# One accumulation over all blocks for layer 1's expert outputs, with four PSUM banks held for it

## The chip, the cores and the metric

One core of one Trainium2 chip runs the whole program. The metric is device time in microseconds (us), one execution of the kernel from start to end; lower is better. Everything is float32 (partly in the float32r form that the TensorE takes at its quicker rate), and the profile names the engines PE (TensorE's matmuls), PEld (its weight loads), DVE (VectorE), ACT (ScalarE), POOL (GpSimd) and SP (the queue that issues nearly all weight loads from memory).

## What is computed

Two layers of a transformer over 256 tokens and 256 context tokens of width 1024. Each layer is modulation, attention, an output projection with a layer norm, then a mixture of experts (MoE) with a second layer norm. In layer 1 only the 256 tokens are left. The part that matters here, cut to its core:

```python
def moe(h, w_router, b_router, w_gate, w_up, w_down):
    ...   # 16 experts in 4 groups; each token picks the best group and its top 2 experts, with weights `gates`
    g = jnp.einsum('...d,edf->...ef', h, w_gate)
    u = jnp.einsum('...d,edf->...ef', h, w_up)
    a = jax.nn.silu(g) * u * gates[..., None].astype(h.dtype)
    return jnp.einsum('...ef,efd->...d', a, w_down)

x = layer_norm(ALPHA * x + g2 * moe(h2, ...), ln_g[l, 1], ln_b[l, 1])
```

## The kernel before

**Blocks.** The kernel doesn't compute all experts for all tokens. Each expert has a slot with a capacity (CAPS, line 39), each slot is cut into blocks of 128, 64 or 32 rows (cut, line 53), and a block computes its expert for the tokens that were routed to it. Layer 1 has 13 slots: three static ones of 32 rows, then ten dynamic ones of 192, 32, 32, 64, 64, 96, 128, 64, 32 and 32 rows in that order, 15 blocks in all (192 is 128 + 64, 96 is 64 + 32). Expert weights (gate, up and down, 2 MB each) come through a ring of twelve tiles of 1 MB; a load is issued on SP when the tile's earlier contents have been used by PE. A loop behind it (overflow, line 1534) takes rows that no slot had room for; here its condition is false and it is skipped.

**One block of layer 1** (step, line 1449) is, in program order: products (line 1226: gate and up products into the PSUM role "acc", L1247 for 32 or 64 rows, L1232 and L1234 for 128), copied out by ACT (L1250); hidden (line 1253: PE transposes through PSUM role "tr", L234; a sigmoid on ACT, L1270; two multiplications on DVE, L1271 and L1272, the second of which writes aT); flush, which is put (line 1331) of the block before; down (line 1275: the product of aT with the down weights into "acc", L1290 or L1284); and put_out's steps (DVE L1326, ACT L1327, DVE L1328) that scale the rows and split them into a high and a low part, yh and yl. The next block's products follow on PE without a wait for these.

**put** scatters a block's rows back to the 256 tokens with matmuls. dt is a one-hot matrix (DVE, L1339, one buffer), and for each of two token tiles t and two column halves n it takes a bank of PSUM role "c" (two buffers), adds the products with yh and yl in it (L1346), and adds the bank to the token rows xs on DVE (L1349). So each block has four such additions, 15 blocks have 60, and the third group of a put waits until the first bank has been read.

**Look-ups and picking.** Which tokens a block takes is found by ranks: block_index (line 1146) makes one-hot matrices dd on DVE (L1159, two buffers), multiplies them on PE into PSUM role "ix" (look_up, L1172) and copies the result out (L1179, L1180). This is done in five batches, the last three (4, 6 and 2 blocks) beside the first blocks. pick (line 1298) gathers up to 128 tokens for a group of blocks with matmuls through "tr" (L1311), copied out by ACT (L1313).

**What sets the order.** The program is not run in the order written: a scheduler at build time orders each engine's instructions by program position among those that it takes to be ready, and gives out a tile's buffers as they come free in its own estimate of time. On the chip each engine then runs its list in order. PSUM has eight banks. In layer 1's MoE the roles hold "acc" 3, "tr" 2, "ix" 1 and "c" 2 (phase, line 191).

Of the kernel before, what the change touches and what calls it, by code (L numbers as in the profile page):

```python
# [10 lines left out]
F32R = mybir.dt.float32r  # L11
# [10 lines left out]
P = 128  # L22
# [120 lines left out]
class K:  # L143
# [47 lines left out]
    def phase(self, kind):  # L191

        if self.c_pp:
            self.c_pp()
        g = self.tc.tile_pool(name=f"pp{self.npp}", bufs=1, space=PSUM)
        self.npp += 1
        self.pp = g.__enter__()
        self.c_pp = lambda: g.__exit__(None, None, None)
        if kind == "attn":
            self.pmap = {"s": ("s", 2), "s2": ("s", 1), "tr": ("tr", 2), "o": ("o", 1), "acc": ("acc", 2), "m": ("m", 1)}  # L200
        else:
            self.pmap = {"acc": ("acc", 4), "tr": ("tr", 3), "ix": ("ix", 1)} if kind == "moe0" else \
                {"acc": ("acc", 3), "tr": ("tr", 2), "ix": ("ix", 1), "c": ("c", 2)}

    def warm(self, n, role, after=None, mark=None):

# [1121 lines left out]
            nc.vector.tensor_sub(yl[:, cs], t, yh[:, cs])  # L1328
        return (yh, yl), out

    def put(self, ys, R, tok, T):

        nc = self.nc
        W = D * R // P
        nj = P // R
        m = self.const(f"jm{R}")
        dt = self.sp.tile([P, nj, P * T], F32R, name="dt", tag="dt", bufs=1)
        for j in range(nj):
            nc.vector.tensor_scalar(dt[:, j], self.const("iota")[:, 0:P * T], tok, m[:, j:j + 1], op0=ALU.is_equal, op1=ALU.mult)  # L1339
        for t in range(T):  # L1340
            for n in range(2):
                ps = self.psum([P, 512], "c")
                w = min(W, 512)
                for c in range(512 * n, 512 * n + 512, w):
                    for i in range(2):
                        nc.tensor.matmul(ps[:, c % 512:c % 512 + w], dt[:, c // W, P * t:P * t + P], ys[i][:, c % W:c % W + w],  # L1346
                                         start=i == 0, stop=i == 1, skip_group_check=True)
                x = self.xs[:, t, 512 * n:512 * n + 512]
                nc.vector.tensor_add(x, x, ps)  # L1349

    def moe(self, l, T, h2d, yd, rp, prep):

        nc = self.nc
# [6 lines left out]
        def onehots(blks):  # L1360

            n = sum(R for _, _, R in blks)
            dd = self.sp.tile([P, T, n], F32R, name="ddr", tag="ddr", bufs=2)
            o = 0
            for sc, r0, R in blks:
                nc.vector.tensor_tensor(dd[:, :, o:o + R], self.const("iota")[:, r0:r0 + R][:, None, :].to_broadcast([P, T, R]),
                                        self.rt["Rs"][:, :, sc:sc + 1].to_broadcast([P, T, R]), op=ALU.is_equal)
                o += R
            return dd
# [59 lines left out]
                    n += R  # L1429
            return out  # L1430

        todo, held = [], []

        def run1(grs, xt0=None, last=False):

            for g in grs:
                xt, xt0 = xt0 or self.pick(onehots([x[:3] for x in g]), T), None
                while todo:
                    step()
                o = 0  # L1440
                for sc, r0, R, load in g:
                    todo.append((xt[:, :, o:o + R], R, load))
                    o += R
            while last and todo:
                step()
            if last:
                flush()

        def step():
            xt, R, load = todo.pop(0)  # L1450
# [8 lines left out]
            self.down(aT, R, wd, out)  # L1459
            held.append((y, R, x))  # L1460

        def flush():
            while held:
                self.put(*held.pop(0), T)

        NS = NE - ndyn(l)
        early = [self.expert_load(l, *s[:2]) for s in slots[:NS]] if l else []
# [6 lines left out]
        n = self.block_index(l, T, slots[:1], 0, ixs)  # L1474
        if l == 0:
            self.warm(3, "acc", self.looked)
        n = self.block_index(l, T, slots[1:NS], n, ixs)
# [3 lines left out]
        if l:  # L1481
            run1(gs, xt0)
        else:
            run(slots[:NS])
            settle()
        self.route_b(l, T, rp)
        for lo, hi in ((NS, NS + 3), (NS + 3, NS + 8), (NS + 8, len(slots))) if l else ((NS, NS + 2),):
            n = self.block_index(l, T, slots[lo:hi], n, ixs)
        if l:
            self.route_c(l, T, rp)  # L1490
            while len(todo) > KEEP:
                step()
            run1(gd, last=True)
            return
# [3 lines left out]
        for j, (lo, hi) in enumerate(zip(cuts, cuts[1:])):  # L1498

            up = min(hi + 3, len(slots))  # L1500
            if up > seen:
                n = self.block_index(l, T, slots[seen:up], n, ixs)
# [31 lines left out]
    def overflow(self, l, T, h2d, yd, prep):  # L1534

        tc, nc, a = self.tc, self.nc, self.a
# [4 lines left out]
        tok = self.const(f"tok{l}", T, 4 + 2 * l)  # L1541
        iota = self.const("iota")
        with tc.If(v > 0):
# [3 lines left out]
            with tc.For_i(0, NE, 1) as e, tc.tile_pool(name=f"ov{l}", bufs=2) as vp:  # L1547
                fl = vp.tile([1, T], I32, name="fl")
                nc.sync.dma_start(fl, fid[bass.ds(e, 1)])
                for b in range(T):  # L1550
                    fv = nc.values_load(fl[0:1, b:b + 1], min_val=0, max_val=512)
                    with tc.If(fv > 0):
                        rs = vp.tile([P, T, T], F32, name="rs")
                        nc.sync.dma_start(rs.rearrange("p b t -> p (b t)"), rod[bass.ds(e, 1)].rearrange("o p x -> (o p) x"))
                        kk = vp.tile([P, T], F32, name="kk")
                        nc.sync.dma_start(kk, k2d[bass.ds(e, 1)].rearrange("o p t -> (o p) t"))
                        rh = vp.tile([P, T, 4 + 2 * l], BF, name="rh")
                        nc.vector.tensor_copy(rh, tok)
                        if l == 0:
                            self.second(rh[:, :, 3:4], kk[:, :, None], T)  # L1560
                        else:
                            k3 = vp.tile([P, T], F32, name="k3")
                            self.pieces(lambda i: rh[:, :, 1 + 2 * i], kk, k3)
                        dd = vp.tile([P, T, P], BF, name="dd")
                        eq = (iota[:, 0:P][:, None, :].to_broadcast([P, T, P]), rs[:, b][:, :, None].to_broadcast([P, T, P]))
                        nc.vector.tensor_tensor(dd, *eq, op=ALU.is_equal)
                        pi = self.psum([P, 1, 2], "ix")
                        self.look_up(pi[:, 0, :], dd, rh, T, l)
                        ix = [vp.tile([P, 1], F32 if l else I32, name=f"ix{i}") for i in range(2)]
                        if l == 0:  # L1570
                            self.finish_index(l, *ix, pi, None, None)
                            xg = vp.tile([P, D], F32, name="xg", bufs=1)
                            nc.vector.memset(xg, 0.0)
                            self.gather(xg, ix[0], P, h2d, NT)
                            xt = self.xgT(xg, P)
                        else:
                            self.finish_index(l, *ix, pi, None, None)
                            ddr = self.sp.tile([P, T, P], F32R, name="ddr", tag="ddr", bufs=2)
                            nc.vector.tensor_tensor(ddr, *eq, op=ALU.is_equal)
                            xt = self.pick(ddr, T)  # L1580

                        def part(nm):
                            kp = 4 if nm == "w_down" else 8
                            n = 4096 // kp
                            rows = "(k p)" if nm == "w_down" else "(p k)"
                            s = a[nm][l][bass.ds(e, 1)].rearrange(f"o {rows} f -> p (o k) f", p=P)

                            def get(k):
                                w = self.ep.tile([P, n], F32, name="wv" + nm, tag="xt" if kp == 4 else "gu")
                                nc.sync.dma_start(w, s[:, k, :])  # L1590
                                return w
                            return get
                        aT = self.hidden(self.products(xt, P, part("w_gate"), part("w_up")), P)
                        wd = part("w_down")
                        y, out = self.rows_out(P) if l == 0 else self.put_out(P, ix[1])
                        pss = [self.psum([P, 512]) for _ in range(2)]
                        for k in range(4):
                            w = wd(k)
                            for n in range(2):
                                nc.tensor.matmul(pss[n], aT[:, k, :], w[:, 512 * n:512 * n + 512], start=k == 0, stop=k == 3)  # L1600
                        for n in range(2):
                            out(pss[n], slice(512 * n, 512 * n + 512))
                        if l == 0:
                            self.scatter(y, ix[1], P, yd, NT)
                        else:
                            self.put(y, P, ix[0], T)

    def combine_load(self, t, T, yd):
        NT = P * T
# [277 lines left out]
```

## Time and profile before

| what | value |
|---|---|
| median of 3 runs | 1063.53 us (1056.98 to 1065.07) |
| the profiled execution | 1061.43 us, its span 1059.6 us |
| PE busy over the span | 979.2 us, 92% |
| DVE busy over the span | 507.3 us, 48% |
| ACT busy over the span | 259.9 us, 25% |
| HBM traffic | 272 GB/s over the span |

The span is the time from the first to the last profiled instruction; what lies around it is 1.8 us. The profile is one execution. PE's busy time has modelled ends, because matmuls overlap in the pipeline: the distance from one start to the next tells what a matmul costs, and a gap before a matmul together with the engine that ended it tells what PE waited for. The granted clock (PEclk) is TensorE's clock as a share of its full 2.4 GHz. Layer 1's MoE lies at the end, from about 820 us to 1047 us of the span.

### The profile page before, as it was taken

The numbers are of one execution on the slowest core, as the hardware profiler recorded it, in microseconds if no ns is written. First come the engines' busy times: TensorE is split into PE (matmuls) and PEld (weight loads), VectorE is DVE, ScalarE is ACT, GpSimd is POOL, SyncE is SP. The second block draws the span as 40 slices with busy tenths as digits, with TensorE's granted clock in tenths as the row PEclk, the third lists the DMA queues.
The fourth block names the chain that finished last, engine by engine and source line by source line (L and its number), as shares of the span: only waits on it lengthen the run. The fifth ranks groups of instructions, "written<-read, shape, count | busy, mean of one in ns | idle before, by whom it ended". The sixth has DMA issues, their size and how long they took to land. (4 is left out here: it accounts for less than half of the span.)

```text
span 1059.6 us, 15578 instructions
## 1 busy us (share of the span) xinstructions
PE 979.2 (92%) x5918; PEld 533.2 (50%) x5918; DVE 507.3 (48%) x1368; ACT 259.9 (25%) x685; POOL 86.0 (8%) x90
## 2 busy tenths in 40 slices
PE   4799999989899899999999997998999999999994
PEld 1466557667544444544444443443653665544542
DVE  2524555665747833331100105879838742533346
ACT  2433343553412111101111211423413111111110
POOL 0000000000102303111111110111003000000001
PEclk9799999999999999999999899999999889999997
DMA  8899761201265199997999986769634692999991
GB/s 313 298 350 330 258 214 58 80 24 57 105 239 214 63 392 401 408 414 292 390 402 401 358 301 248 315 245 405 263 140 136 252 418 79 417 418 376 363 353 47
DMA packets 76937, 286.99 MB, mean 271 GB/s; under 512 B 12449, under 2 KB 27441, under 8 KB 55604
## 3 DMA queue, kind: packets, MB, share of 16 engines
q1 hardware_dynamic: 71600, 268.13, 65.4%
q0 software_dynamic: 4272, 15.08, 4.0%
q10 hardware_dynamic: 980, 2.66, 0.6%
q8 instruction: 51, 0.84, 0.3%
q14 instruction: 34, 0.28, 0.1%
HBM read 279.77 MB, written 8.69 MB: 272 GB/s over the span
## 5 line engine op out<-in xcount | busy, mean ns | idle before, releaser
L1247 PE MATMUL acc<-wring,xt 128*32 128x256 f32 (+1 forms) x1440 | 140.2, 436 | 0.5 <-ACT xt L1223 0.5
L1247 PEld LDWEIGHTS acc<-wring,xt 128*32 128x32 f32 (+1 forms) x1440 | 59.0, 118 | 73.1 <-issue 49.7
L855 PE MATMUL acc<-wring,oT 128*128 128x512 f32 x192 | 89.2, 598 | 0.3 <-DVE y L857 0.3
L1290 PE MATMUL acc<-wring,aT 128*32 128x256 f32 (+1 forms) x720 | 70.7, 436 | 6.5 <-DVE aT L1272 4.2
L459 PE MATMUL acc<-swh,hT 128*128 128x384 f32 x192 | 68.2, 355 | 3.9 <-ACT v L581 3.5
L460 PE MATMUL acc<-swl,hT 128*128 128x384 f32 x192 | 67.6, 352 | 0.0
L1349 DVE TENSOR_TENSOR xs<-xs,c 128x512 f32<-128x512 f32 x60 | 40.4, 684 | 54.6 <-PE c L1346 54.5
L461 PE MATMUL acc<-swh,hT 128*128 128x384 f32 x192 | 66.2, 345 | 0.0
L523 PE MATMUL acc<-wring,hT 128*128 128x512 f32 x128 | 58.8, 593 | 0.0
L1284 PE MATMUL acc<-wring,aT 128*128 128x512 f32 x128 | 57.1, 597 | 0.5 <-DVE aT L1261 0.4
L1232 PE MATMUL acc<-wring,xt 128*128 128x512 f32 x128 | 56.7, 596 | 0.0
L1234 PE MATMUL acc<-wring,xt 128*128 128x512 f32 x128 | 56.2, 592 | 0.0
L410 PE MATMUL m<-wring,cT 128*32 128x512 f32 x256 | 44.3, 660 | 12.4 <-DMA wring<-in_w_mod_dram 12.4
L855 PEld LDWEIGHTS acc<-wring,oT 128*128 128x128 f32 x192 | 33.9, 190 | 33.0 <-issue 31.4
L1290 PEld LDWEIGHTS acc<-wring,aT 128*32 128x32 f32 (+1 forms) x720 | 27.8, 117 | 38.1 <-issue 20.7
L370 POOL TENSOR_TENSOR mv<-ve,nhalf 128x1 f32<-128x1 f32 x12 | 18.3, 1529 | 330.9 <-DVE ve L369 263.6
L1250 ACT COPY gu<-acc 128x256 f32<-128x256 f32 (+1 forms) x27 | 12.0, 444 | 122.5 <-PE acc L1247 122.5
L459 PEld LDWEIGHTS acc<-swh,hT 128*128 128x128 f32 x192 | 36.4, 189 | 9.5 <-issue 4.5
L1234 PEld LDWEIGHTS acc<-wring,xt 128*128 128x128 f32 x128 | 24.3, 190 | 30.6 <-issue 30.4
L1232 PEld LDWEIGHTS acc<-wring,xt 128*128 128x128 f32 x128 | 23.8, 190 | 28.3 <-issue 27.6
L461 PEld LDWEIGHTS acc<-swh,hT 128*128 128x128 f32 x192 | 36.3, 189 | 3.0 <-issue 3.0
L460 PEld LDWEIGHTS acc<-swl,hT 128*128 128x128 f32 x192 | 36.4, 190 | 2.4 <-issue 2.4
(354 smaller groups left out, 1527.9 us busy)
## 6 DMA issues: line engine op xcount, KB each, us to landing
wring<-in_w_gate_dram SPq DMA_DIRECT2D x58, 1024.0 KB, 14.4
wring<-in_w_up_dram SPq DMA_DIRECT2D x58, 1024.0 KB, 15.3
wring<-in_w_down_dram SPq DMA_DIRECT2D x58, 1024.0 KB, 14.2
wring<-in_w_mod_dram SPq DMA_DIRECT2D x48, 1024.0 KB, 8.1
wring<-in_w_in_even_dram SPq DMA_DIRECT2D x24, 256.0 KB, 4.4
wring<-in_w_in_odd_dram SPq DMA_DIRECT2D x6, 1024.0 KB, 11.4
wring<-in_w_out_even_dram SPq DMA_DIRECT2D x4, 1024.0 KB, 5.1
wring<-yd SPq DMA_DIRECT2D x4, 1024.0 KB, 5.8
```

What stands on the lines that cost most here:

```text
L410: nc.tensor.matmul(ps[32 * j:32 * j + 32, :], lhs(k), w[k][:, 512 * j:512 * j + 512], start=k == 0, stop=k == len(w) - 1, tile_position=(0 ...
L459: mm(ps, xh, wh, start=first, stop=False)
L460: mm(ps, xh, wl, start=False, stop=False)
L461: mm(ps, xl, wh, start=False, stop=last)
L523: self.nc.tensor.matmul(ps, h[:, k, :], w(k), start=k == 0, stop=k == 7)
L855: mm = nc.tensor.matmul(ps, oT[:, k, P * t:P * t + P], w[n](k), start=k == 0, stop=k == 7)
L1232: nc.tensor.matmul(pg, xt[:, k, :], gate(k), start=k == 0, stop=k == 7)
L1234: nc.tensor.matmul(pu, xt[:, k, :], up(k), start=k == 0, stop=k == 7)
L1247: nc.tensor.matmul(ps[R * j:R * j + R, :], xt[:, k, :], src[:, W * jj:W * jj + W], start=k == 0, stop=k == 7, tile_position=(0, R * j), sk ...
L1284: nc.tensor.matmul(ps, aT[:, k, :], w(k)[:, 512 * n:512 * n + 512], start=k == 0, stop=k == 3)
L1290: self.last_mm = nc.tensor.matmul(ps[R * j:R * j + R, :], aT[:, k, :], w(k)[:, W * j:W * j + W], start=k == 0, stop=k == 3, tile_position= ...
L1349: nc.vector.tensor_add(x, x, ps)
```

## The change

Layer 1's put no longer takes a bank for each product and adds it to xs. The first put takes four banks (two token tiles by two halves), every later put adds its products to the same four, and only the last put closes them and adds them to xs, with four additions in all. To pay for it "c" gets four banks, "acc" goes from three to two, and "ix" loses its own bank: look-ups take the two banks of "tr". The one-hot matrix dt gets a second buffer. Layer 0 and the overflow path compute as before.

```diff
-                {"acc": ("acc", 3), "tr": ("tr", 2), "ix": ("ix", 1), "c": ("c", 2)}
+                {"acc": ("acc", 2), "tr": ("tr", 2), "ix": ("tr", 2), "c": ("c", 4)}
...
-    def put(self, ys, R, tok, T):
+    def put(self, ys, R, tok, T, sums, last):
...
-        dt = self.sp.tile([P, nj, P * T], F32R, name="dt", tag="dt", bufs=1)
+        dt = self.sp.tile([P, nj, P * T], F32R, name="dt", tag="dt", bufs=2)
...
+        first = not sums
+        if first:
+            sums.extend([self.psum([P, 512], "c") for _ in range(2)] for _ in range(T))
         for t in range(T):
             for n in range(2):
-                ps = self.psum([P, 512], "c")
                 w = min(W, 512)
                 for c in range(512 * n, 512 * n + 512, w):
                     for i in range(2):
-                        nc.tensor.matmul(ps[:, c % 512:c % 512 + w], dt[:, c // W, P * t:P * t + P], ys[i][:, c % W:c % W + w],
-                                         start=i == 0, stop=i == 1, skip_group_check=True)
-                x = self.xs[:, t, 512 * n:512 * n + 512]
-                nc.vector.tensor_add(x, x, ps)
+                        nc.tensor.matmul(sums[t][n][:, c % 512:c % 512 + w], dt[:, c // W, P * t:P * t + P], ys[i][:, c % W:c % W + w],
+                                         start=first and i == 0 and c == 512 * n, stop=last and i == 1, skip_group_check=True)
+                if last:
+                    x = self.xs[:, t, 512 * n:512 * n + 512]
+                    nc.vector.tensor_add(x, x, sums[t][n])
...
-                flush()
+                flush(True)
...
-        def flush():
+        def flush(last=False):
             while held:
-                self.put(*held.pop(0), T)
+                self.put(*held.pop(0), T, sums, last)
...
-                            self.put(y, P, ix[0], T)
+                            self.put(y, P, ix[0], T, [], True)
```

## Rows read from the trace of the kernel before

**Rows 1.** Windows by stage: length, busy us (instructions) per engine, PEclk, DMA share, GB/s.
```profile
842.00:856.00 14.00, 13.93 (x160) 10.52 (x162) 10.84 (x44) 1.59 (x5) 0.00 (x0) 0.76 1.02 415
...
880.70:898.00 17.30, 17.24 (x88) 10.46 (x88) 6.90 (x11) 3.00 (x5) 0.00 (x0) 1.00 0.00 1
898.00:962.00 64.00, 62.00 (x466) 33.18 (x464) 26.87 (x57) 8.91 (x19) 0.00 (x0) 1.00 1.00 405
962.00:1042.70 80.70, 77.50 (x540) 39.47 (x536) 32.98 (x67) 9.95 (x21) 0.00 (x0) 1.00 0.81 318
1042.70:1046.70 4.00, 2.77 (x16) 2.13 (x16) 2.98 (x5) 0.00 (x0) 0.00 (x0) 1.00 0.02 4
```

**Rows 2.** Groups by line, 840 to 1060 us: busy, mean ns, idle before, releaser.
```profile
L1349 DVE TENSOR_TENSOR xs<-xs,c 128x512 f32<-128x512 f32 x60 | 40.4, 684 | 54.6 <-PE c L1346 54.5
```

**Rows 3.** Waits, 856 to 1042.6 us: waiter, releaser, us in total, times, longest.
```profile
PEld acc L1290 <- DVE aT L1272: 4.7, 6, 1.1
PEld c L1346 <- DVE xs L1349: 3.6, 11, 0.5
PE acc L1290 <- DVE aT L1272: 2.9, 6, 0.7
PEld acc L1247 <- DMA wring<-in_w_up_dram: 1.6, 2, 0.8
PEld acc L1290 <- PE c L1346: 1.5, 2, 0.7
```

**Rows 4.** Timeline of one put beside a 64-row block: start us, us, engine line.
```profile
901.82 0.40 PE L1346 MATMUL c<-yl,dt 128*128 128x512 f32 x1
...
902.05 0.39 PE L1346 MATMUL c<-yh,dt 128*128 128x512 f32 x1
...
902.51 0.60 PE L234 MATMUL tr<-ident,gu 128*128 128x128 f32 x4
...
903.15 0.38 ACT L1270 ACTIVATE sgs<-tr 128x256 f32<-128x256 f32 x1 [0.94 <-PE tr L234]
...
903.56 0.42 DVE L1271 TENSOR_TENSOR sgs<-sgs,tr 128x256 f32<-128x256 f32 x1
...
903.90 0.68 DVE L1349 TENSOR_TENSOR xs<-xs,c 128x512 f32<-128x512 f32 x1
...
904.50 0.42 DVE L1272 TENSOR_TENSOR aT<-sgs,tr 128x256 f32<-128x256 f32 x1
...
904.97 3.65 PE L1290 MATMUL acc<-wring,aT 128*64 128x512 f32 x16 [0.65 <-DVE aT L1272]
```

**Rows 5.** Windows, PE alone, first put matmul to first down matmul.
```profile
859.20:862.23 3.03, 3.03 (x25) 1.00 1.03 407
...
912.13:915.40 3.27, 2.85 (x14) 1.00 1.06 428
...
935.88:939.65 3.77, 3.01 (x22) 1.00 1.00 414
...
1016.69:1020.17 3.48, 2.85 (x14) 1.00 1.02 424
```

**Rows 6.** Timeline, a 128-row block's down product.
```profile
883.51 1.12 PE L1284 MATMUL acc<-wring,aT 128*128 128x512 f32 x2
...
884.95 6.17 PE L1284 MATMUL acc<-wring,aT 128*128 128x512 f32 x14
```

**Rows 7.** Timeline, the stretch with the last look-ups.
```profile
847.98 0.28 DVE L1272 TENSOR_TENSOR aT<-sgs,tr 128x128 f32<-128x128 f32 x1
...
850.32 0.58 PE L1346 MATMUL c<-yh,dt 128*128 128x256 f32 x1
...
853.34 2.34 PE L1311 MATMUL tr<-ddr,h2s 128*128 128x128 f32 x16
```

**Rows 8.** The up loads issued at 920.8 and 921.8 us.
```profile
L155 SPq DMA_DIRECT2D wring<-in_w_up_dram x2: 333/381/429, 920.8 to 921.8; - x2
...
DMA to landing us min/median/max: 18.8/19.6/20.4
```

**Rows 9.** Timeline of PE, products of the block that uses these.
```profile
943.15 7.04 PE L1247 MATMUL acc<-wring,xt 128*64 128x512 f32 x32
```

More of the change, by code (lines that the diff above doesn't have):

```diff
@@ L1430, in groups @@
             return out
-        todo, held = [], []
+        todo, held, sums = [], [], []
         def run1(grs, xt0=None, last=False):
```

## Prediction

> **What bounds the kernel now.** I read the page first: PE is busy 92% of the span, DVE 48%, so the DVE work that the change removes counts only where PE stands still for it. Next the windows by stage [rows 1]. From 856 to 1042.7 us PE is busy nearly all the time and at its full clock (only 842 to 856 has a granted clock of 0.76, a mixture of the levels 1.2 and 2.4 GHz: at half speed for about 48% of 14 us, 6.7 us). DMA is saturated from 898 to 962 us (share 1.00) but carried nothing from 880.7 to 898 us, so the ring of weight tiles fills up and then waits for PE. The waits confirm who leads [rows 3]: PE's weight loads waited 1.6 us for the up weights in this whole stretch, but 4.7 us for aT from DVE and 3.6 us for a put's bank to be read by DVE. So the stage is paced by PE, with short stops for DVE at one place, the put. The group of additions [rows 2] is 60 of 684 ns, 40.4 us in all, but DVE idles 54.6 us ahead of them: most of the 40 us is hidden already.
>
> **What the change removes.** 56 of the 60 additions go, 56 x 0.684 = 38.3 us of DVE time. What of it lies on PE's path is read at one put beside a 64-row block [rows 4]. Put matmuls of 512 columns start 0.23 us apart (901.82, 902.05), so a put's eight cost 1.84 us; narrower blocks have sixteen of half the width, which I take at the same 1.84 us. The transposition (L234) ends at 903.11, the sigmoid at 903.53, DVE's first multiplication (L1271) runs 903.56 to 903.98. The second (L1272) needs nothing more, but an addition stands ahead of it in DVE's list (903.90), and it starts at 904.50; the down product starts at 904.97. Without the addition L1272 follows L1271 after the same 0.34 us by which these overlapping DVE instructions follow each other (903.56 to 903.90), so down starts near 904.97 - 0.60 = 904.37. PE's own work (1.84 us of put and about 0.5 us of transposition) is 2.4 us of such a stretch's 3.48 [rows 5] and doesn't hold it back. Gain: 0.55 us, rounded down for the semaphore.
>
> The same for the other blocks [rows 5]:
> - 64-row blocks, five of them: windows between the first put matmul and the first down matmul are 3.48 to 3.50 us in four (the row at 1016.69 stands for them) and 3.77 us in one (935.88). With 0.55 taken off, the four need 2.9 us; the one then needs the same, a gain of 0.9: 4 x 0.55 + 0.9 = 3.1 us.
> - 32-row blocks that follow a 64-row one, two of them, 3.26 and 3.27 us (912.13): the chain of a 32-row block is shorter (transposition, sigmoid and multiplications are half as wide), so PE's work decides: 1.84 + 0.35 = 2.2 us. Gain 2 x 1.05 = 2.1 us.
> - The other four 32-row blocks, up to 3.26 us (first at 859.20, 3.03 us): their windows also hold three to six picking matmuls that have to be done anyway, so 1.84 + 0.35 + 0.4 = 2.6 us is left in the first: 4 x 0.4 = 1.6 us.
> - 128-row blocks, two: four put matmuls are stuck between the second and third down matmul [rows 6], because their bank came late. The first two down matmuls take 2 x 0.43 us from 883.51, so the third could start at 884.37 and starts at 884.95: 2 x 0.58 = 1.15 us.
> - The last put (the window from 1042.7) [rows 1]: PE's sixteen matmuls no longer wait for banks, but four additions still follow one another, 4 x 0.684 = 2.7 us of the window's 4.00, and the first can't start before the first bank is full, some 1 us in: 0.3 us is left to win.
>
> Sum 3.1 + 2.1 + 1.6 + 1.15 + 0.3 = 8.2 us. Its bounds are the waits themselves [rows 3]: 2.9 us, where only the pauses of PE proper for aT count, and 4.7 + 3.6 + 1.5 = 9.8 us, where every wait of a weight load on aT or on the puts counts too. I take 8.2 because it comes from the starts of matmuls, which aren't modelled.
>
> **What it adds or moves.** The second buffer of dt lets L1339 run earlier in DVE gaps; it costs nothing, since DVE has the 54.6 us of idle time [rows 2]. "acc" with two buffers: a block of 32 or 64 rows needs one for its products and one for down, a block of 128 two and two, and each is read within 1 us of its last matmul, while the next user of that buffer starts a whole product later (3.65 us for the down product [rows 4]); nothing there, up to 1 us against. No DMA is issued differently: SP's loads follow PE.
>
> The look-ups in the banks of "tr" do cost something, in one place: the last three batches, 841 to 848.6 us, run beside a 32-row block's transposition, whose aT comes only at 847.98 because DVE is full of one-hot matrices, and beside the first picking matmuls. Before, those had "tr" for themselves and 16 of 32 picking matmuls ran between the look-ups. With a batch in one bank and that transposition in the other, picking has to wait until 848, behind the down product, where the other 16 take 2.27 us (853.34 to 855.61, part of it at the low clock) [rows 7]: 2.3 us later. Against it, the four put matmuls that cut the down product in two (850.32 to 851.48, waiting for a bank) run before it in gaps, 1.2 us, and one addition leaves DVE's list ahead of the one-hot matrices, 0.6 us. Net +0.5 us. The bounds: if PE has no other filler, its clock stays low for as long again, half of 6.7 us or 3.4 us more, and with both transposition and picks behind the look-ups some 4 us of work at half speed, +8; if products of the next block fill the gap and the clock doesn't fall at all, 3.4 + 0.6 = -4. I take +0.5, nearest to the rows as they stand.
>
> A rule speaks against this. The put's matmuls at 850.32 [rows 7] are such a case: they waited for a bank while DVE was behind. The Trainium skill, Perfetto Trace Analysis, section Optimizing Tensor Performance (Matmuls), says independent groups should rotate through different PSUM banks so that the copy out of one overlaps the next group's matmuls. By that rule fewer banks for "acc", "tr" and look-ups lose in the early stretch; the second rival below is what that would do here, worked out from rows.
>
> Sum: -8.2 + 0.5 = -7.7 us. The profiled execution took 1061.43 us (span 1059.6 and 1.8 around it): 1053.7 us. The median of the runs is 2.1 us above that execution, which gives 1055.8; I say 1055.
>
> **Rivals.**
> - Weights become late. From 898 us DMA is saturated, and PE gets 2.9 us nearer to it by 943 (0.55 + 1.05 + 0.4 + 0.9). The block at 943.15 [rows 9] needs the up tiles issued at 920.8 and 921.8, which took 18.8 and 20.4 us [rows 8]: landed at 939.6 and 942.2. The first is needed at once, 3.5 us of slack, the second half way through the products, 4.5 us. So it holds, barely. If loads are late instead, the 3.9 us won between 898 and 962 (these four and the next blocks' 0.45 and 0.55) are lost: 1053.7 + 3.9, 1058.
> - The shared banks eat half: transposition and picks behind the look-ups, +6 in place of +0.5: 1059 to 1061.
> - Slower: the scheduler gives "tr" to the look-ups so early that also the first block's transposition (833 us) waits for them. Then that block's down product (1.9 us), put (1.84), both transpositions (0.7) and the picks (1.8) move behind 848.6 us, 6.3 us of work, at the low clock 12.6, and the clock's return comes later by 3.4: +16 less 8.2 and the 2 us that the next products fill: 1067. It decides from 8.2 us of early loss on. Against it: DVE has no look-up to copy between 829 and 841, so a bank should be free.
> - Better: the clock doesn't fall in 842 to 856, and early is -4: 1049 to 1050.
>
> **How the numbers follow.** Forecast 0.53 (own range 1051 to 1059), weights late 0.07, shared banks eat half 0.16, slower 0.07, better 0.17. From better to half eaten is 1049 to 1061; with the runs' own scatter of some 4 us either way that shows in the times before, 1047 to 1064. A change of 1% is about what a measurement of this kernel can tell from none, here 10.6 us: faster by more (below 1052.9) needs the better case or the lower end of the forecast, 0.27; slower by more (above 1074.2) only the far end of the slower one, 0.04; the rest, 0.69.
>
> **What would show it.** Right: four additions in place of 60; no wait of the down product on L1272 behind an addition; windows from put to down near 2.9 us for 64-row blocks and 2.2 to 2.6 for 32-row ones; 128-row down products in one piece; weights landed before the products that use them; and the MoE's end near 1039 of the span. Wrong: a window 842 to 856 that grows by several us or has a lower clock, look-up matmuls that wait for ACT's copies out of "tr", waits of L1247 for weights of several us, or picks that all stand in one piece behind the down product.

## The result and the profile after

The median after is 1067.78 us (14 runs, 1063.44 to 1073.39); the kernel before, run beside it, has 1060.12 us (14 runs, 1055.46 to 1065.07). The ratio is 1.0084 with an interval of 1.0064 to 1.0103: the change makes the kernel slower by some 8 us, by 0.8%, clear of the scatter of the runs, where 1055 was predicted with a range up to 1064.

The profiled execution after took 1071.49 us, span 1069.7, 10.1 us more than the profiled execution before. To see where, I cut both spans at events that both have: the first picking matmul (L1311), the first product of the third block, the first matmul of the last put, the end of the last addition.

| stretch | before, us | after, us | difference |
|---|---|---|---|
| start to the first pick | 821.05 | 824.08 | +3.0 |
| first pick to third block's products ("early") | 34.56 | 41.55 | +7.0 |
| third block's products to last put ("late") | 187.09 | 187.73 | +0.6 |
| last put to the end of the last addition | 3.92 | 3.62 | -0.3 |
| from there to the end | 12.94 | 12.68 | -0.3 |

The first stretch is nearly all ahead of layer 1's MoE, where the two programs are the same; its length is 818.5 to 826.7 us over the profiles of all kernels below, in no order that goes with their edits, so 3.0 us lie within its scatter. The 7.0 us of the early stretch is about the difference of the medians (7.7 us). In the late stretch, where 8 us were to be won, nothing was left in the end.

The windows by stage of the kernel before, early and late (length, busy us and instructions per engine, PEclk, DMA share, GB/s):

```profile
821.05:855.61 34.56, 32.31 (x368) 21.96 (x368) 25.81 (x100) 3.66 (x9) 0.00 (x0) 0.80 0.75 291
855.61:1042.70 187.09, 181.82 (x1265) 97.93 (x1264) 73.93 (x157) 25.27 (x52) 0.00 (x0) 1.00 0.81 326
```

The same of the kernel after, then one short window inside the early stretch and one inside the late one:

```profile
824.08:865.63 41.55, 31.18 (x369) 21.20 (x369) 25.77 (x102) 3.65 (x9) 0.00 (x0) 0.75 0.61 230
865.63:1053.36 187.73, 180.72 (x1265) 97.49 (x1264) 41.41 (x96) 25.23 (x52) 0.00 (x0) 0.99 0.81 328
840.64:854.30 13.66, 8.25 (x111) 5.23 (x115) 10.12 (x51) 0.28 (x1) 0.00 (x0) 0.50 0.44 159
936.20:939.60 3.40, 3.40 (x11) 1.47 (x12) 0.56 (x3) 0.40 (x1) 0.00 (x0) 0.50 1.05 417
```

Early, PE is busy 1.1 us less than before and stands idle 10.4 us (41.55 - 31.18) in place of 2.3: idle time, not more work. The granted clock was lower too (0.75 for 0.80): in the last part of the stretch the lower level (0.50) lasted 13.7 us, from 840.64 to 854.30, and 6.8 us before. But for 8.0 of the 13.7 us, up to 848.63, PE stood idle or did look-ups as their matrices came from DVE; in the rest it was busy 4.6 us, against 6.8 us at the lower level before. So the loss is the idle time. Late, DVE has 61 instructions and 32.5 us less to do, as it should, and the window is no shorter for it.

**Where the early time went.** PE's timeline before; here the first block's transposition (L234) and down product (L1290) stand ahead of the look-ups (L1172), and the second block's products run while PE would wait for them:

```profile
833.38 0.44 PE L234 MATMUL tr<-ident,gu 128*128 128x128 f32 x2 [0.51 <-ACT gu L1250]
834.85 1.93 PE L1290 MATMUL acc<-wring,aT 128*32 128x256 f32 x32 [1.03 <-DVE aT L1272]
836.60 3.62 PE L1247 MATMUL acc<-wring,xt 128*32 128x256 f32 x58
840.86 0.16 PE L1172 MATMUL ix<-RH,dd 128*128 128x2 bf16 x1 [0.64 <-DVE RH L1023]
```

After, same view: the first block's products end at 835.69, and then PE stands still until DVE has made RH for a look-up.

```profile
831.19 4.50 PE L1247 MATMUL acc<-wring,xt 128*32 128x256 f32 x54
842.86 0.16 PE L1172 MATMUL tr<-RH,dd 128*128 128x2 bf16 x1 [7.18 <-DVE RH L1023]
...
847.89 0.69 PE L1172 MATMUL tr<-RH,dd 128*128 128x2 bf16 x12 [0.15 <-DVE dd L1159]
848.63 0.66 PE L234 MATMUL tr<-ident,gu 128*128 128x128 f32 x2
849.08 0.35 PE L1172 MATMUL tr<-RH,dd 128*128 128x2 bf16 x6
850.45 1.08 PE L1290 MATMUL acc<-wring,aT 128*32 128x256 f32 x8 [1.02 <-DVE aT L1272]
```

The waits after, 824 to 865.6 us (waiter, releaser, us in total, times, longest), say the same from both sides: ACT's sigmoid waits 13.2 us for the transposition, and PE 7.2 us for RH.

```profile
ACT sgs L1270 <- PE tr L234: 13.7, 2, 13.2
...
PE tr L1172 <- DVE RH L1023: 7.2, 1, 7.2
```

It is not a bank that is late at 835.7 but a place in the list. PE's matmuls in the order of the built program, from the first block's products on (one matmul of L1247 or L1290 is two records in the trace, so x27 here is x54 there):

```
before: L1247x19 L234x2 L1290x16 L1247x29 L1172x1 ...
after:  L1247x27 L1172x66 L234x2 L1172x6 L1290x16 L1247x32 ...
```

Once look-ups and transpositions draw on the same two banks, 66 look-ups stand ahead of the first transposition; the first of them needs RH, which DVE has ready at 842.8, and everything behind it on PE waits too, the second block's products among them (853.87 after, 836.60 before).

**Where the late gain went.** The group of additions after (us busy, mean ns, idle before) has four of the 60 in [rows 2], of the same length:

```profile
L1352 DVE TENSOR_TENSOR xs<-xs,c 128x512 f32<-128x512 f32 x4 | 2.5, 683 | 0.7 <-PE c L1348 0.7
```

The windows from put to down, PE alone, shrank as forecast, in the order of [rows 5]: 3.03 to 2.42, 3.27 to 2.24, 3.77 to 2.87, 3.48 to 3.01.

```profile
869.22:871.64 2.42, 2.42 (x22) 1.00 1.03 415
...
921.08:923.32 2.24, 2.24 (x14) 1.00 1.04 411
945.30:948.17 2.87, 2.70 (x22) 1.00 1.00 414
1027.08:1030.09 3.01, 2.57 (x14) 1.00 1.00 425
```

Added up over the thirteen blocks from the third on, the time from the start of the last product matmul to the first down matmul fell from 46.13 to 38.86 us, 7.3 us less, and the two 128-row down products became shorter by 1.2 us together (7.01 to 6.44 us each, from first to last start). Against that, 1.9 us more pass between a down product and the next products, mostly because 13 picking matmuls (some 0.12 us each) have moved there from the windows. So 6.6 us were won. But the time from each block's first product to its last rose from 80.0 to 87.3 us, 7.2 us more, in three blocks alone: the second of the 64-row blocks in mid-stretch 10.25 us for 6.44, the last block 6.64 for 4.49, and one 64-row block 7.79 for 6.50. The first two are seen in PE's timeline after:

```profile
951.67 1.02 PE L1247 MATMUL acc<-wring,xt 128*64 128x512 f32 x2
...
953.39 1.19 PE L1348 MATMUL c<-yh,dt 128*128 128x512 f32 x4 [0.71 <-ACT yh L1327]
...
955.43 7.08 PE L1247 MATMUL acc<-wring,xt 128*64 128x512 f32 x30
963.25 0.66 PE L234 MATMUL tr<-ident,gu 128*128 128x128 f32 x4 [0.73 <-ACT gu L1250]
965.33 3.65 PE L1290 MATMUL acc<-wring,aT 128*64 128x512 f32 x16 [0.70 <-issue]
...
1041.30 0.60 PE L1247 MATMUL acc<-wring,xt 128*32 128x256 f32 x4
1042.58 0.73 PE L1348 MATMUL c<-yh,dt 128*128 128x256 f32 x4 [0.68 <-ACT yh L1327]
...
1044.67 3.65 PE L1247 MATMUL acc<-wring,xt 128*32 128x256 f32 x60
```

The put of the block before stands behind the first one or two gate products and ahead of all others. There it waits for ACT's yh (0.71 and 0.68 us), which the other puts of the late stretch find ready, and it is missing behind the products, where it filled PE's wait for the transposition and aT: the 64-row block still has 2.82 us from 962.51, the end of its products, to 965.33. The third block is the window at 936.20 shown above: PE busy in all of it, granted clock 0.50, the lower level (1.2 GHz); 1.3 us. In the last block the kernel before had four of the sixteen put matmuls between products already (1034.63 to 1035.30 of its span), which is why its 4.49 us are more than the 3.28 of other 32-row blocks.

### The profile page after: what moved, and what is told of

It reads as the page before. It is cut to its first block, busy times and chain, and to the rows that moved or that the text cites. A ratio compares the mean times of both kernels' runs of the same rounds, so it can differ in the third digit from the quotient of the medians.

```text
span 1069.7 us, 15522 instructions
## 1 busy us (share of the span) xinstructions
PE 980.5 (92%) x5918; PEld 534.9 (50%) x5918; DVE 474.8 (44%) x1312; ACT 259.8 (24%) x685; POOL 86.0 (8%) x90
## 3 DMA queue, kind: packets, MB, share of 16 engines
q10 hardware_dynamic: 980, 2.66, 0.6%
## 5 line engine op out<-in xcount | busy, mean ns | idle before, releaser
L1247 PE MATMUL acc<-wring,xt 128*32 128x256 f32 (+1 forms) x1440 | 142.3, 441 | 0.5 <-ACT xt L1223 0.5
L1247 PEld LDWEIGHTS acc<-wring,xt 128*32 128x32 f32 (+1 forms) x1440 | 59.0, 120 | 75.7 <-issue 53.5
L1290 PE MATMUL acc<-wring,aT 128*32 128x256 f32 (+1 forms) x720 | 70.5, 436 | 6.2 <-issue 3.4
L459 PE MATMUL acc<-swh,hT 128*128 128x384 f32 x192 | 69.3, 361 | 4.7 <-ACT v L581 4.2
L461 PE MATMUL acc<-swh,hT 128*128 128x384 f32 x192 | 67.4, 352 | 0.0
L1271 DVE TENSOR_TENSOR sgs<-sgs,tr 128x128 f32<-128x128 f32 (+1 forms) x27 | 8.9, 329 | 127.3 <-ACT sgs L1270 127.3
L1290 PEld LDWEIGHTS acc<-wring,aT 128*32 128x32 f32 (+1 forms) x720 | 28.1, 117 | 38.0 <-issue 24.4
L459 PEld LDWEIGHTS acc<-swh,hT 128*128 128x128 f32 x192 | 37.1, 193 | 10.1 <-ACT v L581 4.7
```

The lines of the kernel that those rows point to most:

```text
L459: mm(ps, xh, wh, start=first, stop=False)
L461: mm(ps, xl, wh, start=False, stop=last)
L1247: nc.tensor.matmul(ps[R * j:R * j + R, :], xt[:, k, :], src[:, W * jj:W * jj + W], start=k == 0, stop=k == 7, tile_position=(0, R * j), sk ...
L1290: self.last_mm = nc.tensor.matmul(ps[R * j:R * j + R, :], aT[:, k, :], w(k)[:, W * j:W * j + W], start=k == 0, stop=k == 3, tile_position= ...
```

## Experiments

No kernel below leaves anything out of the computation. Each ratio is against the kernel before, run on the same chip beside it; kernels of different series are compared by these ratios.

**e1_share_only and e2_acc_only: the change's two halves alone, in the kernel before.** Is it the shared banks, or the two accumulators?

```diff
# e1_share_only
-  {"acc": ("acc", 3), "tr": ("tr", 2), "ix": ("ix", 1), "c": ("c", 2)}
+  {"acc": ("acc", 3), "tr": ("tr", 2), "ix": ("tr", 2), "c": ("c", 2)}
# e2_acc_only
+  {"acc": ("acc", 2), "tr": ("tr", 2), "ix": ("ix", 1), "c": ("c", 2)}
-  dt = ... bufs=1)
+  dt = ... bufs=2)
```

> The kernel before with one edit: look-ups take the two banks of tr (acc 3, c 2 and the additions as before, one bank unused). Theory A (the tr banks are given out in program order, so the first block's transposition queues behind the last look-ups): slower than before by about 7 us, ratio 1.0065, nearly all of it between the first picking matmul and the third block's products (34.6 us before, about 41 us here). Rival B (two buffers for acc hold up the products): no change, ratio 1.000, 34.6 us.

> The kernel before with acc at two buffers and dt at two, nothing else. Theory A: within 1.5 us of before, the stretch of 34.6 us within 1.5 us. Rival B: slower by 5 to 7 us, with the second block's products starting some 10 us later.

Sharing alone: 1066.01 us, ratio 1.0080 [1.0053, 1.0107], as much as the whole change. Its windows, early and late, and the stop in PE's timeline:

```profile
823.26:863.15 39.89, 29.20 (x368) 20.34 (x368) 26.92 (x102) 3.65 (x9) 0.00 (x0) 0.79 0.66 245
863.15:1050.23 187.08, 181.87 (x1265) 97.98 (x1264) 73.45 (x152) 25.25 (x52) 0.00 (x0) 1.00 0.82 328
```
```profile
839.49 0.16 PE L1172 MATMUL tr<-RH,dd 128*128 128x2 bf16 x1 [7.51 <-DVE RH L1023]
```

The early stretch has the loss (39.89, 5.3 us more than before, where the change has 7.0) and the late one is that of before (187.08 for 187.09). The rest of the 8.0 us between the medians isn't seen in this one execution. Two accumulators alone: 1060.29 us, 1.0031 [1.0008, 1.0054], 2.3 us over the median before where at most 1.5 were expected. Its profile shows no place for a loss (early 30.70, late 189.65, together 1.3 us less than before), so those 0.3% stay open; they are not the 0.8% sought.

**e3_pin: the change, with each put held behind the last product matmul of the running block.** This adds no wait on the chip (both are on PE), only an order.

```diff
-   nc.tensor.matmul(pu, ...)
+   self.pm = nc.tensor.matmul(pu, ...)      # the same at L1247
...
-   nc.tensor.matmul(sums[t][n]...)
+   x = nc.tensor.matmul(sums[t][n]...)
+   self.tc.add_manual_dep(x.ins, self.pm.ins.name, NOSYNC, ...)
```

> The changed kernel, with every put matmul ordered behind the products of the block it stands beside. Theory A2 (in two places the order built in advance puts a put in front of the products, where PE then waits for yh and later has nothing to fill the wait for aT): faster than the changed kernel by 4 to 6 us, the stretch from the third block's products to the last put 187.7 us there, about 182 to 183 us here. Rival C (weights are late there): no gain, PE waits at the same products for the up weights instead.

1060.94 us, 1.0017 [0.9995, 1.0039]. The two blocks are back to 6.44 and 3.26 us from first to last product; windows early and late, then the 64-row block in one piece:

```profile
826.72:866.85 40.13, 28.50 (x368) 20.09 (x369) 25.71 (x102) 3.65 (x9) 0.00 (x0) 0.79 0.62 232
866.85:1048.35 181.50, 178.65 (x1265) 96.99 (x1264) 41.31 (x96) 25.34 (x52) 0.00 (x0) 0.99 0.85 341
```
```profile
952.93 7.04 PE L1247 MATMUL acc<-wring,xt 128*64 128x512 f32 x32
```

Late 181.50 where the change has 187.73: so the places of the puts cost 6.2 us, somewhat more than the 4 to 6 expected. Some 1.2 us of that the kernel before pays too, in its last block (4.49 for 3.26). The fall of the clock in the other block is still there (7.98 us), so it is not theirs.

**e4_steps_first and e8_before_steps: the steps of the running blocks moved ahead of the last three look-up batches**, in the change and in the kernel before. In program order the first transposition then comes before those look-ups.

```diff
+        while l and len(todo) > KEEP:
+            step()
         for lo, hi in ((NS, NS + 3), (NS + 3, NS + 8), (NS + 8, len(slots))) if l else ((NS, NS + 2),):
             ...
             n = self.block_index(l, T, slots[lo:hi], n, ixs)
-            while len(todo) > KEEP:
-                step()
```

> The changed kernel, with the first two blocks' steps written ahead of the last three batches of look-ups, so that their transpositions ask for tr first. Theory A: faster than the changed kernel by about 7 us, back at the time of before (ratio 0.999 to 1.001 against before); the early stretch goes from 41.6 to about 34 us. Rival D (the look-ups and their DVE chain take PE's time wherever they stand): less than 2 us gained, the loss moves to the third block's products.

> The kernel before with the first two blocks' steps written ahead of the last three batches of look-ups, nothing else (look-ups have their own bank, puts add each block). If the order alone is worth something: ratio 0.996 to 0.998, the stretch to the third small block shorter by 2 to 4 us. If it was only a cure for sharing the banks: 1.000, within 1 us of before.

e4: 1057.66 us, 0.9988 [0.9963, 1.0014]; e8: 1058.47 us, 1.0004 [0.9979, 1.0030], though its one profiled stage was 3.4 us shorter than that of before (218.26 for 221.65 us, early and late together). So by itself the order of the steps is worth nothing that an interval of 0.3% either way could show, and it is worth 1% to a kernel that shares the banks. e4's windows, early and late, and its timeline:

```profile
824.54:847.48 22.94, 20.51 (x277) 13.39 (x277) 19.15 (x81) 2.66 (x7) 0.00 (x0) 0.93 0.71 266
847.48:1041.72 194.24, 187.21 (x1359) 102.41 (x1356) 47.07 (x119) 26.16 (x54) 0.00 (x0) 1.00 0.83 335
```
```profile
847.48 1.05 PE L1247 MATMUL acc<-wring,xt 128*32 128x256 f32 x10
848.50 0.30 PE L1172 MATMUL tr<-RH,dd 128*128 128x2 bf16 x6
848.73 0.64 PE L1247 MATMUL acc<-wring,xt 128*32 128x256 f32 x8
```

Early falls by 18.6 us, late rises by 6.5: the look-ups now stand in sixes among the third block's products, 7.5 us in place of 3.3, and so outside the early stretch, which is why it is far below the 34 us expected. The sum falls by 12.1 us; the ratios differ by 0.96 per cent, some 10 us.

**e5_both: e3's and e4's edits together.**

> The changed kernel with both edits: the first two blocks' steps ahead of the last look-ups, and put matmuls behind the products they stand beside. Theory A with A2: the two gains add, ratio against before 0.992 to 0.994 (about 1051 us where before has 1058); from the third block's products to the last put about 188 us where the first edit alone has 194.25, each 64-row block's wait before the down product about 3.5 us, each 32-row one's 2.6. Rival: the weights become late once the early stretch is short, and 3 us or more of it come back as waits of the products for weights: ratio 0.996 or above.

1049.71 us (6 runs, 1047.03 to 1052.11), 0.9910 [0.9879, 0.9942]: faster than both kernels. The two edits had brought 0.67 and 0.96 per cent of the change's 1.0084; together they bring 1.74, so within the intervals they add up. That is more than the 0.992 to 0.994 expected. Windows, early and late:

```profile
820.55:843.79 23.24, 20.79 (x276) 13.68 (x276) 19.29 (x81) 2.67 (x7) 0.00 (x0) 0.93 0.75 291
843.79:1031.74 187.95, 185.09 (x1359) 102.21 (x1356) 46.90 (x119) 26.27 (x54) 0.00 (x0) 1.00 0.85 343
```

**e6_rotate4: e5_both with an addition for every bank again**, the four banks of "c" taken in turn. What is the accumulation itself worth?

```diff
-                self.put(*held.pop(0), T, sums, last)
+                self.put(*held.pop(0), T, [], True)
```

> As e5_both, but each put closes its four banks and adds them to xs, as before the change (60 additions, with four banks to rotate through). Theory E (what cost PE time were additions ahead of the multiplication that makes aT, in DVE's list): 64-row blocks wait some 4.0 us again before the down product, 32-row ones 3.2, and 5 us or more of the late gain goes. Rival F (what cost it was the wait for one of two banks): as e5_both within 1.5 us.

1055.09 us, 0.9967 [0.9947, 0.9988], 5.4 us above e5_both in the same series (span 4.8 us longer in the profiles). The timeline beside the same 64-row block, e5_both first, then e6_rotate4, where the line of the addition is L1353:

```profile
898.17 0.60 PE L234 MATMUL tr<-ident,gu 128*128 128x128 f32 x4
...
899.22 0.42 DVE L1271 TENSOR_TENSOR sgs<-sgs,tr 128x256 f32<-128x256 f32 x1 [8.57 <-ACT sgs L1270]
...
899.68 0.42 DVE L1272 TENSOR_TENSOR aT<-sgs,tr 128x256 f32<-128x256 f32 x1
...
900.15 1.08 PE L1290 MATMUL acc<-wring,aT 128*64 128x512 f32 x4 [0.45 <-DVE aT L1272]
```
```profile
898.16 0.60 PE L234 MATMUL tr<-ident,gu 128*128 128x128 f32 x4
...
899.21 0.42 DVE L1271 TENSOR_TENSOR sgs<-sgs,tr 128x256 f32<-128x256 f32 x1
...
899.55 0.68 DVE L1353 TENSOR_TENSOR xs<-xs,c 128x512 f32<-128x512 f32 x1
...
900.15 0.41 DVE L1272 TENSOR_TENSOR aT<-sgs,tr 128x256 f32<-128x256 f32 x1
...
900.62 0.65 PE L1290 MATMUL acc<-wring,aT 128*64 128x512 f32 x2 [0.93 <-DVE aT L1272]
```

From transposition to down is 1.98 us without the addition and 2.46 with it, to the hundredth what the kernel before had (902.51 to 904.97, [rows 4]). More banks don't help here; the addition in DVE's list is the cost. From the last product matmul to the first down matmul (starts) 64-row blocks take 4.0 to 4.3 us again, as expected, for 3.4 to 3.6 in e5_both, and from the first 128-row block's products to the last put the profile has 173.18 us for 168.35: the whole 4.8 us of the spans.

**e7_spread and e10_spread2: e5_both with the last two look-up batches moved further back**, so that they don't crowd into the third block's products; e7 puts the first of the two behind the steps of the first 128-row block, e10 ahead of them.

```diff
-        for lo, hi in ((NS, NS + 3), (NS + 3, NS + 8), (NS + 8, len(slots))) if l else ((NS, NS + 2),):
+        for lo, hi in ((NS, NS + 3),) if l else ((NS, NS + 2),):
...
-            run1(gd, last=True)
+            run1(gd, last=True, later=[lambda: None, <second batch>, <third batch>])
```

> As e5_both, with the last two batches of look-ups moved behind the first 128-row block and behind the third small block, so that eight blocks' one-hot matrices leave the crowded stretch. If DVE's list is what holds the third block's products up (7.5 us for 3.3 us of work in e4_steps_first): 2 to 4 us faster than e5_both. If PE only waits for the same look-ups at their new place: no gain.

> As e7_spread, with the two late batches one place earlier, ahead of the first 128-row block's products (14 us of PE work in which DVE is idle) instead of behind its down product. If e7 lost its gain because PE stood waiting for one-hot matrices at the new place: the 64-row block's products start some 27 us after the 128-row block's, as in e5_both (31 in e7), and the whole is 2 to 4 us faster than e5_both, ratio 0.987 to 0.990. If the look-ups cost the same wherever they stand: as e7, 0.995 to 0.998.

e7: 1055.97 us, 0.9970 [0.9947, 0.9993]: not faster than e5_both but slower, by 6.3 us in the same series. At the new place PE waited for DVE's one-hot matrices for two short times (0.29 and 0.24 us), and then its granted clock fell to 0.50:

```profile
888.83 0.30 PE L1172 MATMUL tr<-RH,dd 128*128 128x2 bf16 x6 [0.29 <-DVE dd L1159]
...
890.75 4.72 PE L1311 MATMUL tr<-ddr,h2s 128*128 128x128 f32 x21
```
```profile
890.67:897.50 6.83, 6.83 (x33) 5.39 (x35) 1.19 (x5) 1.18 (x2) 0.00 (x0) 0.50 0.00 0
```

The 64-row block's products start 31.0 us after the 128-row block's there, 26.7 in e5_both and 27.8 in e10. Of these 4.3 us the two waits are 0.5, the look-ups themselves about 1.0 (by the starts of the matmuls), and the clock about 2.3: 21 picking matmuls take 4.72 us, where 26 take 3.07 in e10. The 64-row block's products then take 7.51 us from first to last for 6.50. Over all runs the mean granted clock is 0.969 in e7 and 0.975 in e5_both, so it is not this one execution alone. The second expectation (no gain) came out, but the wait that it names is the smaller part of the loss. What made the clock fall there stays open; ahead of the fall PE did look-ups and picking matmuls, busy 2.66 of the 3.19 us from 887.48 on.

e10: 1048.66 us (11 runs, 1045.47 to 1054.96), 0.9929 [0.9906, 0.9953]. The 2 to 4 us expected over e5_both did not come; the intervals overlap, and the two are as good as equal.

**e9_merge: the change with one shared tile for all three last batches**, so that the look-ups take one bank of the two for the whole time and the transpositions keep the other.

```diff
-        pi = self.psum([P, n, 2], "ix")
+        pi = self.psum([P, n, 2], "ix") if pi is None else pi
```

> The changed kernel, with the last three batches of look-ups in one bank instead of three requests for banks, so that a second bank of tr is free for the first block's transposition. Theory A in its strict form (a bank is given to the transposition only once the look-ups asked for earlier have theirs, and they get theirs with their first matmul, which waits for DVE's ranks): at most 2 us faster than the changed kernel, ratio against before 1.006 to 1.008, the early stretch 40 us or more. Rival G (there were simply too few banks for three batches and a transposition): about 7 us faster, ratio 1.000 to 1.002, the early stretch about 34 us.

1064.44 us, 1.0078 [1.0052, 1.0105]. The early window and the timeline:

```profile
823.19:864.19 41.00, 31.57 (x369) 21.52 (x369) 25.74 (x102) 3.66 (x9) 0.00 (x0) 0.75 0.62 233
```
```profile
842.12 0.16 PE L1172 MATMUL tr<-RH,dd 128*128 128x2 bf16 x1 [7.34 <-DVE RH L1023]
842.15 0.67 PE L234 MATMUL tr<-ident,gu 128*128 128x128 f32 x2
```

Now the transposition stands behind one look-up, not 66, its bank is free, and it still waits for the same RH, as the strict form expected. So it isn't that two banks are too few for the look-ups and a transposition at the same time: one look-up ahead of it in PE's list is enough.

## Why the prediction was wrong

Two steps failed, of about the same size. Between the -7.7 us forecast and what the profiles show lie some 15 us: 6.5 in the early term, 8.5 in the late one.

**The early term (+0.5; measured about +7) had its path wrong.** It took the loss to be where the trace of before shows look-ups, from 841 us on, "beside a 32-row block's transposition". It lies before that: at 833 us the first block's transposition, down product and the second block's products had all been ahead of the look-ups. That sharing a role's buffers also sets the order of those who draw on it was not in the term: 66 look-ups came to stand ahead of that transposition, and PE waited 7.2 us for RH.

**The rival "slower" named this** (the first block's transposition given its bank behind the look-ups), and its time, 1067, came out. I gave it 0.07 because "DVE has no look-up to copy between 829 and 841, so a bank should be free". e9_merge shows why that is no argument: the bank is free and the transposition waits, since PE's list is in order and the look-up ahead of it waits for RH. Its time is right by luck: it priced the early loss near 14 us (16 less the 2 that products fill), twice what it was, and kept the 8.2 us of the late gain, of which nothing was left.

**The late term (-8.2; measured +0.3) was right in what it removed, and left out what the put's own place costs.** Forecast windows of 2.9, 2.2 to 2.6 and 2.6 us came out at 3.01, 2.24 and 2.42; in all, 6.6 us were won there, beside 7.9 forecast without the last put (0.3, measured 0.3). Part of the difference is the picking matmuls that the forecast kept inside the windows of the 32-row blocks: they now stand behind the down products. e6_rotate4 shows that the addition in DVE's list makes the difference, by the step that [rows 4] gave it: 0.48 us where I took 0.55. The 128-row blocks' forecast of 0.58 each came to 0.35 and 0.45 (from one block's products to the next block's). What was not in the sum is that two puts would change their place in PE's list (6.0 of the 7.2 us that products lost; the other 1.3 are the fall of the clock). With every put behind the products, e3_pin has 181.50 us in the late stretch, 5.6 less than before, with that fall of the clock still in it. The put had been costed as work that PE does anyway; its 1.84 us are free only in the gap in front of down. Why the built order puts those two elsewhere isn't settled: their program order was not altered. The kernel before has one put of the two partly so already, in its last block.

**Weights late** did not happen: the up tiles of that 64-row block were issued at 928.8 and 931.3 us, took 20.3 us each, and the products start at 951.67; in the waits of the late stretch no wait for a load is above 0.3 us. **The rule of rotating banks** that the prediction took from the Trainium skill (Perfetto Trace Analysis, Optimizing Tensor Performance (Matmuls)) pointed at the right stretch but for a reason that the runs don't bear out: for the look-ups it isn't the number of banks (e9_merge), and for the puts, rotating four banks loses 5.4 us against holding them (e6_rotate4 against e5_both).

**The base** moved too: 1063.53 us by three runs, 1060.12 by fourteen.

## What to carry to other kernels

Before two uses are put on one pool of buffers, list who asks for it in program order, and what the first instruction of each asker waits for: on an engine that runs its list in order, a free bank doesn't help an instruction that stands behind a waiting one. After a change that a scheduler orders, compare the order of the bottleneck's list with the one before, block by block; a gain that is seen in each window can be lost again by a single filler put where there is no gap. Both were a few lines to mend (from 1.0084 to 0.9910 of the time before), and without the order list either could have passed for a cost of the accumulation.

## What the runs showed of the hardware that was not expected

The granted clock fell to 0.50 at 936.20 for 3.40 us while PE was busy in all of those 3.40 us and also ahead of them, with the picking matmuls from 932.95 on, inside a stretch that has 0.99 over its length. The same block was slow in e3_pin (7.98 us from first to last product) and e9_merge (8.10), and normal in e5_both (6.50), where the same picking matmuls stand ahead of it. What PE did before differs between e3_pin and e5_both by the early stretch alone, but no run takes that apart. In e7_spread the clock stayed at 0.50 for 6.83 us with PE busy in all of them. Elsewhere there was idle time ahead of a fall: in the early stretch of the change PE had stood idle since 835.69 when the clock fell at 840.64.
